# A two-block transformer on one core: how the end of each expert layer adds up its rows

## The chip, the cores and the metric

The kernel runs on one core of one Trainium2 chip. The metric is the device time of one execution in microseconds (us). The profiler's trace covers one execution; its engines are TensorE (PE, with its weight loads as PEld), VectorE (DVE), ScalarE (ACT), GpSimd (POOL) and SyncE (SP), which issues most DMAs.

## The reference, cut to what matters

512 tokens of width 1024 pass a first block (a state space mixer beside attention, then a convolutional feed-forward layer) and a second block of two layers. Layer 0 has gated linear attention, layer 1 sparse attention ("NSA"); each is followed by a mixture of 16 experts, of which a token uses two, and by layer norms:

```
for i in range(DEPTH_2):                       # 2 layers
    h = gla_mixer(x, ...) if i % 2 == 0 else nsa_mixer(x, ...)
    x = layer_norm(DN_ALPHA * x + h, ln_g[i, 0], ln_b[i, 0])
    f = moe_ffn(x, moe_w_router, moe_b_router, moe_w_gate[i], moe_w_up[i], moe_w_down[i])
    x = layer_norm(DN_ALPHA * x + f, ln_g[i, 1], ln_b[i, 1])

def layer_norm(x, g, b):
    mu = mean(x); var = mean(square(x - mu))
    return (x - mu) * rsqrt(var + LN_EPS) * g + b
```

In `moe_ffn` a token's two expert outputs are weighted and added. The change touches that sum and the layer norm behind it, the last line of the loop, in both layers.

## The kernel before, in words

The residual stream lies in SBUF as four row tiles `xt[0..3]` of 128 tokens x 1024 floats. The kernel is recorded through a framework with a scheduler that puts each engine's instructions in an order and adds the semaphores; buffers are pages of one arena (`pg`), the raw 1 MB weight pages being a ring of ten ("wr"). PSUM pool `p2` has three tiles of two banks (128x1024 floats), `p1` two of one bank.

The expert stage runs expert by expert. `up` makes the hidden rows, `turn` transposes them (`ht`), and `down` multiplies by the down weights into PSUM (`psy`, three matmuls for each product since numbers are split in a high and a low part; lines 394 to 396, operands split by an ACT cast and a DVE subtraction, line 369). Outputs of experts 0 to 13 are copied from PSUM (L1508) and scattered by GpSimd to DRAM, into `yd`, two rows of 1024 for each token. Experts 14 and 15 come too late for that way: their output is weighted on ACT (L1515) and stays in SBUF, with a 0/1 matrix `m` that says which token each row belongs to (`self.late`).

`combine` then makes z = residual + weighted rows + the two late experts. SP loads the rows `y` of each row tile from `yd` (L1459, four loads of 1 MB), behind the layer norm's gain and bias (L1165). On TensorE (L1574, L1581), in plain float32, a row tile gets identity x `xt`, `m14` x `yo14`, and where the tile is in `by_pe`, diag(weight) x `y` for both rows of a token (`dw`, made by DVE in L1540 to 1544); expert 15 comes last (L1581). `by_pe` is (0, 1) in layer 0 and (0, 1, 2, 3) in layer 1; the other tiles' rows are added on DVE beforehand by `mac`, two 128x1024 instructions (L1463). Then for each tile: `bn_stats` x2 and `bn_aggr` on DVE (L1591, L1592), a square root on ACT (L1593), a Newton step on DVE (L1600 to L430), and the scaling: in layer 0 on ACT (L1178), in layer 1 two DVE instructions with gain and bias (L1595, L1608) and the store of the output.

In layer 0 the next stage starts inside: `x4_tile` transposes a normalised tile (L1748), applies gain and bias while copying out of PSUM (L1756 on ACT, L1758 on DVE), splits it, and multiplies it by `w_n1` (tile name `n`); behind the four tiles the same input goes through `w_n2` and `w_n4` (tile name `tm`). `w1_split` splits the three pages of `w_n1` between the steps. DVE's order in `combine` is that of the code; the other engines' order is the scheduler's.

Of the kernel before, what the change touches and what calls it, by code (L numbers as in the profile page):

```python
# [268 lines left out]
def build(ctx, tc, I, out, dbg=None):  # L269
# [890 lines left out]

    def load_gb(gi):
        g_ = sb(2048, "lngb")
        gb = [g_[:, :1024], g_[:, 1024:]]
        for j in range(2):
            nc.sync.dma_start(out=gb[j], in_=I['lngb'][gi:gi + 1, j * 1024:(j + 1) * 1024].to_broadcast([P, 1024]))  # L1165
        return gb
# [24 lines left out]
    class Layer:  # L1191
        def __init__(self, l, by_pe):
            self.l, self.by_pe = l, by_pe
            self.xd = dr.tile([S, 1024], F32, tag=f"xd{l}", name=f"xd{l}")
            self.yd = dr.tile([2 * S, 1024], F32, tag=f"yd{l}", name=f"yd{l}")
# [300 lines left out]
        def down(self, e, hs):  # L1496
# [6 lines left out]
            for k in range(2):  # L1503
                for nh in range(2):
                    mm3(psy[:, nh], (hh[:, k * P:(k + 1) * P], hl[:, k * P:(k + 1) * P]), wt.next(512), k == 0, k == 1)
            yo = sb(1024, "ysb", bufs=3)
# [14 lines left out]
        def experts(self):  # L1521
# [31 lines left out]
            for t in reversed(range(4)):  # L1553
                ar.rings[f"y{t}"] = (4, [ar.rings["wr"][1].pop()])
            drop("gh", "gl", "hs", "hhl", "wr", "wh", "wl")
            wt.bufs = 2

        def combine(self, done=None, between=None):


            self.gb = load_gb(2 * self.l + 1)
            eps = small("epsl", (1,))
            V.memset(eps, LN_EPS / ALPHA ** 2)

            def early(t):

                ps = p2("late")
                for nh in range(2):
                    c = slice(nh * 512, (nh + 1) * 512)
                    a = [(ident, xt[t][:, c]), (self.late[0][0][:, t * P:(t + 1) * P], self.late[0][1][:, c])]  # L1570
                    if t in self.by_pe:
                        a += [(self.dw[:, t, k], self.y[t][:, k * 1024 + nh * 512:k * 1024 + (nh + 1) * 512]) for k in range(2)]
                    for i, (l_, r_) in enumerate(a):
                        TE.matmul(ps[:, nh], l_, r_, start=i == 0, stop=False)  # L1574
                if t in self.by_pe:
                    drop(f"y{t}")
                return ps

            def last(t):
                for nh in range(2):  # L1580
                    TE.matmul(z[t][:, nh], self.late[1][0][:, t * P:(t + 1) * P], self.late[1][1][:, nh * 512:(nh + 1) * 512], start=False, stop=True)  # L1581

            z = [early(0), early(1)]
            last(0)
            last(1)
            with tc.manual_schedule(engines={mybir.EngineType.DVE}):
                for t in range(5):
                    if t < 4:
                        bs, mv, rs = (small(n, (w,), bufs=2) for n, w in (("bs", 12), ("mv", 2), ("lrs", 2)))
                        for j in range(2):  # L1590
                            V.bn_stats(bs[:, 6 * j:6 * j + 6], z[t][:, j])  # L1591
                        V.bn_aggr(mv, bs)  # L1592
                        A.activation(rs[:, 0:1], mv[:, 1:2], AF.Sqrt, bias=eps)  # L1593
                        if not done:
                            V.scalar_tensor_tensor(v2(xt[t]), z[t], mv[:, 0:1], v2(self.gb[0]), op0=ALU.subtract, op1=ALU.mult)  # L1595
                        if between:
                            between(t)
                        if t < 2 and t + 2 not in self.by_pe:
                            self.mac(t + 2)
                        V.reciprocal(rs[:, 0:1], rs[:, 0:1])  # L1600
                        V.tensor_scalar(bs[:, 0:1], mv[:, 1:2], LN_EPS / ALPHA ** 2, -0.5, op0=ALU.add, op1=ALU.mult)
                        run(newton(rs[:, 0:1], bs[:, 0:1], bs[:, 1:2]))
                        if done:
                            V.scalar_tensor_tensor(rs[:, 1:2], mv[:, 0:1], -1.0, rs[:, 0:1], op0=ALU.mult, op1=ALU.mult)
                            normalize(v2(xt[t]), z[t], rs)
                        else:
                            for c in (slice(0, 1024),) if t < 3 else (slice(0, 512), slice(512, 1024)):
                                V.scalar_tensor_tensor(xt[t][:, c], xt[t][:, c], rs[:, 0:1], self.gb[1][:, c], op0=ALU.mult, op1=ALU.add)  # L1608
                                nc.sync.dma_start(out=out[t * P:(t + 1) * P, c], in_=xt[t][:, c])
                    if t > 0 and done:  # L1610
                        done(t - 1)
                    if t in (1, 2):
                        z.append(early(t + 1))
                        last(t + 1)
            drop("ysb", "xg")


# [79 lines left out]

    L0 = Layer(0, (0, 1))
    L0.start()
# [28 lines left out]
    def w1_split():  # L1728
        n = 1680 if len(w1) < 2 else 1120
        w1.append((sb(1680, "w1h", FR, 3)[:, :n], sb(1680, "w1l", FR, 3)[:, :n]))  # L1730
        for j in split(st.get()[:, :n], *w1[-1]):
            if len(w1) > 1:
                after(j, L0.last)

    w1_split()
    x4h, x4l = [], []
    kcd = dr.tile([S, 512], F32, tag="kcd", name="kcd")
# [355 lines left out]
```

## Time and profile before

| | |
|---|---|
| median of three runs | 1930.62 us (1928.56 to 1931.67) |
| the profiled execution | 1927.89 us, of which the span is 1925.8 us |
| busy: PE, PEld, DVE, ACT | 94%, 78%, 63%, 45% of the span |
| mean granted TensorE clock | 0.965 |
| layer 0's combine in the trace | about 1249 to 1328 us |
| layer 1's combine | about 1876 to 1922 us |

Times in the trace are microseconds from the start of the span; a row of the timeline has the start, the length, and in brackets how long the engine was idle before it and which instruction's end released it.

### The profile page before, as it was taken

What the parts mean: (1) busy time and instruction counts of PE and PEld (TensorE: products, weight loads), DVE (VectorE), ACT (ScalarE), POOL (GpSimd) and SP (SyncE); (2) the same over time, 40 slices, a digit from 0 to 9 for tenths busy, and PEclk for the clock granted to TensorE, in tenths of its full rate; (3) what the DMA queues carried; (4) which work ended last, traced back from release to release, by engine and by line L of the source; (5) the groups of instructions that cost most, each with busy time, mean ns of one, the idle gap of its engine ahead of it and who ended that gap; (6) DMA issues with size and microseconds to landing.
All of it is one profiled execution on the core that took longest, in us unless ns stands there. A gap on an engine that the chain in (4) does not pass through costs nothing. (4 is left out here: it accounts for less than half of the span.)

```text
span 1925.8 us, 27564 instructions
## 1 busy us (share of the span) xinstructions
PE 1806.3 (94%) x10879; PEld 1506.3 (78%) x10879; DVE 1211.6 (63%) x2304; ACT 874.9 (45%) x1394; POOL 148.6 (8%) x128
## 2 busy tenths in 40 slices
PE   8899999899999999999999699979998999869997
PEld 7899877798899888877888588748886777748873
DVE  7755358776555543235348789954437777678994
ACT  4233346433333322243214388834225665638880
POOL 2310000021000000000000122200000000012220
PEclk9999999899999999999989799989998999879999
DMA  5434222242222232372226599552241002639953
GB/s 193 113 115 136 83 88 66 67 159 105 88 88 102 96 123 104 111 254 89 88 66 241 193 328 380 214 220 82 78 136 40 2 1 88 237 144 330 381 212 130
DMA packets 68279, 277.87 MB, mean 144 GB/s; under 512 B 21923, under 2 KB 24499, under 8 KB 42032
## 3 DMA queue, kind: packets, MB, share of 16 engines
q1 hardware_dynamic: 52032, 255.30, 37.1%
q0 software_dynamic: 8640, 16.00, 2.2%
q10 hardware_dynamic: 7472, 4.76, 1.1%
q8 instruction: 87, 1.43, 0.3%
q14 instruction: 48, 0.39, 0.1%
HBM read 258.01 MB, written 37.24 MB: 153 GB/s over the span
## 5 line engine op out<-in xcount | busy, mean ns | idle before, releaser
L369 ACT CAST pg<-pg 128x1024 fp32r<-128x1024 f32 (+2 forms) x437 | 428.2, 1004 | 556.8 <-PE mm L395 224.4
L369 DVE TENSOR_TENSOR pg<-pg,pg 128x1024 fp32r<-128x1024 f32 (+2 forms) x437 | 504.2, 1176 | 278.3 <-ACT pg L369 264.7
L394 PE MATMUL mm<-pg,pg 128*128 128x258 f32 (+2 forms) x1504 | 483.8, 322 | 1.3 <-ACT pg L888 0.7
L396 PE MATMUL mm<-pg,pg 128*128 128x258 f32 (+2 forms) x1504 | 481.7, 321 | 3.3 <-DVE pg L369 3.3
L395 PE MATMUL mm<-pg,pg 128*128 128x258 f32 (+2 forms) x1504 | 481.6, 320 | 0.0
L394 PEld LDWEIGHTS mm<-pg,pg 128*128 128x128 f32 x1504 | 286.4, 191 | 27.7 <-ACT pg L886 2.7
L396 PEld LDWEIGHTS mm<-pg,pg 128*128 128x128 f32 x1504 | 285.7, 190 | 24.1 <-DVE pg L369 3.9
L395 PEld LDWEIGHTS mm<-pg,pg 128*128 128x128 f32 x1504 | 286.3, 190 | 21.2 <-issue 0.4
L360 DVE TENSOR_TENSOR pg<-mm,pg 128x256 f32<-128x256 f32 (+3 forms) x138 | 66.3, 510 | 137.9 <-PE mm L396 137.8
L394 PE MATMUL psh<-pg,pg 128*128 128x512 f32 x256 | 105.8, 413 | 7.1 <-ACT pg L369 7.1
L395 PE MATMUL psh<-pg,pg 128*128 128x512 f32 x256 | 105.8, 413 | 3.3 <-DVE pg L369 3.3
L396 PE MATMUL psh<-pg,pg 128*128 128x512 f32 x256 | 103.8, 406 | 0.2 <-DVE pg L369 0.2
L395 PE MATMUL tm<-pg,pg 128*128 128x512 f32 x192 | 76.7, 400 | 3.0 <-DVE pg L369 3.0
L396 PE MATMUL tm<-pg,pg 128*128 128x512 f32 x192 | 75.2, 392 | 0.0
L394 PE MATMUL tm<-pg,pg 128*128 128x512 f32 x192 | 74.6, 399 | 0.3 <-ACT pg L369 0.3
L1990 ACT ACTIVATE pg<-ns,nmx 128x512 f32<-128x512 f32 (+3 forms) x128 | 66.3, 531 | 10.1 <-DVE nmx L1986 5.6
L360 DVE TENSOR_TENSOR pg<-pg,pg 128x512 f32<-128x512 f32 (+11 forms) x99 | 52.3, 549 | 23.7 <-ACT pg L675 9.4
L394 PEld LDWEIGHTS psh<-pg,pg 128*128 128x128 f32 x256 | 49.9, 195 | 18.5 <-ACT pg L369 8.3
L1986 DVE TENSOR_REDUCE nmx<-ns 128x2 f32<-128x1024 f32 (+3 forms) x48 | 50.0, 1042 | 19.2 <-PE ns L1983 19.0
L395 PEld LDWEIGHTS psh<-pg,pg 128*128 128x128 f32 x256 | 49.9, 195 | 15.1 <-DVE pg L369 4.8
L360 DVE TENSOR_TENSOR pg<-pg 128x64 f32<-128x64 f32 (+8 forms) x127 | 48.5, 403 | 17.4 <-ACT pg L1033 15.4
L396 PEld LDWEIGHTS psh<-pg,pg 128*128 128x128 f32 x256 | 49.6, 194 | 11.1 <-DVE pg L369 0.8
(460 smaller groups left out, 3018.0 us busy)
## 6 DMA issues: line engine op xcount, KB each, us to landing
pg<-in_w_moe_dram SPq DMA_DIRECT2D x96, 1024.0 KB
pg<-in_w_up_dram SPq DMA_DIRECT2D x22, 1024.0 KB
pg<-in_w_dn_dram SPq DMA_DIRECT2D x11, 1024.0 KB
pg<-in_w_g_dram SPq DMA_DIRECT2D x8, 1024.0 KB
yd<-zd SPq DMA_DIRECT2D x16, 512.0 KB
pg<-in_w_go_dram SPq DMA_DIRECT2D x8, 1024.0 KB
pg<-yd SPq DMA_DIRECT2D x8, 1024.0 KB
pg<-in_w_n_dram SPq DMA_DIRECT2D x8, 1024.0 KB
```

The lines of the kernel that those rows point to most:

```text
L360: return (eng or V).tensor_tensor(o, a, b, op=op)
L369: return A.copy(h, src), V.tensor_tensor(l, src, h.bitcast(F32), op=ALU.subtract)
L394: TE.matmul(o, a[0], b[0], start=start, stop=False)
L395: TE.matmul(o, a[0], b[1], start=False, stop=False)
L396: return TE.matmul(o, a[1], b[0], start=False, stop=stop)
L1986: V.tensor_reduce(mx, sc, axis=AX.X, op=ALU.max, negate=True)
L1990: A.activation(pp[:, r, br], sc[:, r, br], AF.Exp, bias=mx[:, r, br:br + 1], accum_out=se[:, r, br:br + 1])
```

## The change

All four row tiles of both layers now get their rows by `mac` on DVE; `by_pe` and `dw` are gone. TensorE multiplies only the two late experts (`late_rows`), ordered behind the last `psy` matmul. In layer 0 the residual stays on DVE, which adds the PSUM tile into `xt` (`add`), takes its statistics from SBUF and normalises from SBUF. The last layer has a function of its own, `combine_last`: TensorE adds the residual by the identity, ACT makes the sum of z, the sum of (z - mean)^2 and its root, DVE the scalings. In layer 0 the three loads of `w_n1` are issued ahead of the row loads and gain and bias behind them. The gain and bias of `xt` itself (`affine`) is ordered behind the last split of `x4_tile`.

```diff
@@ class Layer, experts
-                if e == 14:
-                    self.dw = self.xg[2].rearrange("p (t k n) -> p t k n", t=4, k=2)
-                    for t in self.by_pe:
-                        tt(self.dw[:, t], ident.unsqueeze(1).to_broadcast([P, 2, P]), bc(self.wts[:, :, t], P), ALU.mult)
+            early = 0
+            if self.l == 0:
+                st.ahead(3)
+                early = 3
+            else:
+                self.load_gb2()
+                early = 1
             for t in range(4):
                 self.y.append(sb(2048, "wr", F32, WM))
                 ld = self.load(t, self.y[t])
...
+        def late_rows(self, t, ps, own=False):
+            for i, (m, yo) in enumerate(self.late):
+                for nh in range(2):
+                    c = slice(nh * 512, (nh + 1) * 512)
+                    last = TE.matmul(ps[nh], m[:, t * P:(t + 1) * P], yo[:, c], start=i == 0, stop=i == 1 and not own)
+                    after(last, self.done_by)
+                    if own and i == 1:
+                        TE.matmul(ps[nh], ident, xt[t][:, c], start=False, stop=True)
...
+            def add(t):
                 for nh in range(2):
+                    z = xt[t][:, nh * 512:(nh + 1) * 512]
+                    tt(z, z, ps[t][nh], ALU.add)
+            ps = [late(t) for t in range(3)]
             with tc.manual_schedule(engines={mybir.EngineType.DVE}):
+                self.mac(0)
                 for t in range(5):
                     if t < 4:
+                        add(t)
...
-                            V.bn_stats(bs[:, 6 * j:6 * j + 6], z[t][:, j])
+                            V.bn_stats(bs[:, 6 * j:6 * j + 6], xt[t][:, 512 * j:512 * (j + 1)])
...
+                        if t < 3:
+                            self.mac(t + 1)
+                        self.root(rs[:, 0:1], mv[:, 1:2], bs)
+                        V.scalar_tensor_tensor(rs[:, 1:2], mv[:, 0:1], -1.0, rs[:, 0:1], op0=ALU.mult, op1=ALU.mult)
+                        normalize(xt[t], xt[t], rs)
+                    between(t)
+                    if t > 0:
                         done(t - 1)
+                    if t == 1:
+                        ps.append(late(3))
...
+        def combine_last(self):
...
+            def total(t):
+                z[t] = p2("late")
+                self.late_rows(t, [z[t][:, 0], z[t][:, 1]], True)
+                A.activation(v2(waste), z[t], AF.Copy, accum_out=ss[:, t:t + 1])
+            def mean(t):
+                V.tensor_scalar(nm[:, t:t + 1], ss[:, t:t + 1], -1.0 / D, None, op0=ALU.mult)
+                A.activation(v2(waste), z[t], AF.Square, bias=nm[:, t:t + 1], accum_out=ss[:, 4 + t:5 + t])
+                A.activation(rs[:, t:t + 1], ss[:, 4 + t:5 + t], AF.Sqrt, scale=1.0 / D, bias=eps)
+            with tc.manual_schedule(engines={mybir.EngineType.DVE}):
+                self.mac(0)
+                self.mac(1)
+                total(0)
+                total(1)
+                mean(0)
+                for t in range(4):
+                    V.scalar_tensor_tensor(v2(xt[t]), z[t], nm[:, t:t + 1], v2(self.gb[0]), op0=ALU.add, op1=ALU.mult)
+                    if t < 2:
+                        self.mac(t + 2)
+                        total(t + 2)
+                    if t < 3:
+                        mean(t + 1)
+                    r, v = rs[:, t:t + 1], ss[:, 4 + t:5 + t]
+                    V.tensor_scalar(v, v, 1.0 / D, None, op0=ALU.mult)
+                    self.root(r, v, b[:, 2 * t:2 * t + 2])
+                    for c in (slice(0, 1024),) if t < 3 else (slice(0, 512), slice(512, 1024)):
+                        V.scalar_tensor_tensor(xt[t][:, c], xt[t][:, c], r, self.gb[1][:, c], op0=ALU.mult, op1=ALU.add)
+                        nc.sync.dma_start(out=out[t * P:(t + 1) * P, c], in_=xt[t][:, c])
...
@@ x4_tile and behind it
-            split(f[:, hf], x4h[t][:, hf], x4l[t][:, hf])
+            x4_last.append(split(f[:, hf], x4h[t][:, hf], x4l[t][:, hf])[1].ins.name)
...
-        affine(xt[t], L0.gb, V)
+        for i in affine(xt[t], L0.gb, V):
+            after(i, x4_last[-1])
```

First place: SP's loads at the start of layer 0's combine, before. `lngb` is gain and bias, `yd` the rows, 128x1680 the pages of `w_n1`, 128x2048 those of `w_n2` and `w_n4`.

```order
L334 DMA pg_92<-in_w_moe_dram 128x2048
L1165 DMA pg_8640<-in_lngb_dram 128x1024 x2
L1459 DMA pg_94<-yd_7634 128x2048
L1459 DMA pg_96<-yd_7634 128x2048
L1459 DMA pg_7171<-yd_7634 128x2048
L1459 DMA pg_7110<-yd_7634 128x2048
L334 DMA pg_8638<-in_w_n_dram 128x1680
L334 DMA pg_92<-in_w_n_dram 128x1680
L334 DMA pg_102<-in_w_n_dram 128x1680
L334 DMA pg_8638<-in_w_n_dram 128x2048
L334 DMA pg_92<-in_w_n_dram 128x2048
L334 DMA pg_102<-in_w_n_dram 128x2048
```

The same loads in the changed kernel:

```order
L334 DMA pg_96<-in_w_n_dram 128x1680
L334 DMA pg_7171<-in_w_n_dram 128x1680
L1460 DMA pg_7110<-yd_7634 128x2048
L1460 DMA pg_102<-yd_7634 128x2048
L1460 DMA pg_7119<-yd_7634 128x2048
L1460 DMA pg_7628<-yd_7634 128x2048
L1165 DMA pg_8638<-in_lngb_dram 128x1024 x2
L1836 DMA pg_132<-in_w_c_dram 128x384
L1836 DMA pg_132<-in_c_ropec_dram 128x64
L1836 DMA pg_132<-in_c_pe_dram 128x16
L334 DMA pg_7628<-in_w_n_dram 128x2048
L1822 DMA kcd<-pg_6402 128x512
```

The three `w_n1` loads moved from behind the rows to ahead of them, gain and bias from ahead to behind, and two small loads stand ahead of the next weights.

Second place: TensorE around the last expert's `psy` in layer 0, before (a row with x2 is two instructions).

```order
L1499 MATMUL ht<-c_ident,pg_7017 128x128 x2
L394 MATMUL psy<-pg_430,pg_8987 128x512
L395 MATMUL psy<-pg_430,pg_8987 128x512
L1574 MATMUL late<-pg_7017,c_ident 128x512
L1574 MATMUL late<-pg_132,pg_7064 128x512
L1574 MATMUL late<-pg_132,c_ident 128x512
L1574 MATMUL late<-pg_132,pg_7064 128x512
L396 MATMUL psy<-pg_430,pg_8987 128x512
L394 MATMUL psy<-pg_430,pg_8987 128x512
L395 MATMUL psy<-pg_430,pg_8987 128x512
L396 MATMUL psy<-pg_430,pg_8987 128x512
L394 MATMUL psy<-pg_483,pg_8987 128x512
```

And in the changed kernel, from the last `psy` on, with `x4T` the transposes and `late_10259`, `late_10260` two one-bank tiles:

```order
L394 MATMUL psy<-pg_483,pg_8987 128x512
L395 MATMUL psy<-pg_483,pg_8987 128x512
L396 MATMUL psy<-pg_483,pg_8987 128x512
L1576 MATMUL late<-pg_132,pg_7064 128x512 x2
L1576 MATMUL late<-pg_7094,pg_7064 128x512 x2
L1576 MATMUL late<-pg_132,pg_7064 128x512 x2
L1576 MATMUL late<-pg_7094,pg_7064 128x512 x2
L1576 MATMUL late<-pg_132,pg_7064 128x512 x2
L1576 MATMUL late<-pg_7094,pg_7064 128x512 x2
L1799 MATMUL x4T<-c_ident,pg_7017 128x128 x8
L1576 MATMUL late_10259<-pg_132,pg_7064 128x512
L1576 MATMUL late_10260<-pg_132,pg_7064 128x512
```

The four float32 matmuls inside `psy` are gone; three row tiles of four matmuls each follow it, then the first transposes.

Third place: DVE at the end of the kernel with the semaphores that an instruction waits for, in the changed kernel from the first `mac` on. L1464 is `mac`, L1643 the mean's sign, L1654 the scaling by the gain that reads PSUM (`late`), L1664 the last one.

```order
L1464 SCALAR_TENSOR_TENSOR pg_7017<-pg_10699,wts,pg_7017 128x1024 [waits DMAHW0_49]
L1464 SCALAR_TENSOR_TENSOR pg_7017<-pg_10699,wts,pg_7017 128x1024 [waits DVE_49]
L1464 SCALAR_TENSOR_TENSOR pg_132<-pg_11453,wts,pg_132 128x1024 [waits DMAHW1_49]
L1464 SCALAR_TENSOR_TENSOR pg_132<-pg_11453,wts,pg_132 128x1024 [waits DVE_49]
L1643 TENSOR_SCALAR lnm<-lss 128x1 [waits Activation_49]
L1654 SCALAR_TENSOR_TENSOR pg_7017<-late,lnm,pg_7628 128x1024 [waits DMAHW6_49,PE_49,Activation_49]
L1464 SCALAR_TENSOR_TENSOR pg_7060<-pg_11524,wts,pg_7060 128x1024 [waits DMAHW2_49]
L1464 SCALAR_TENSOR_TENSOR pg_7060<-pg_11524,wts,pg_7060 128x1024 [waits DVE_49]
L1643 TENSOR_SCALAR lnm<-lss 128x1
L1661 TENSOR_SCALAR lss<-lss 128x1 [waits Activation_49]
L1585 RECIPROCAL lrt<-lrt 128x1
L1586 TENSOR_SCALAR lbs<-lss 128x1 [waits DVE_49]
```

And ACT there, from the weighting of expert 15 on: L1640 is the sum, L1644 the squares, L1645 the root.

```order
L1517 ACTIVATE pg_6402<-psy,sw 128x1024 [waits DMASW6_49,PE_49]
L1640 ACTIVATE pg_7017,lss<-late 128x1024 [waits DMASW1_49,PE_49]
L1640 ACTIVATE pg_7017,lss<-late 128x1024 [waits PE_49,Activation_49]
L1644 ACTIVATE pg_7017,lss<-late,lnm 128x1024 [waits DVE_49,Activation_49]
L1645 ACT_TABLE_LOAD
L1645 ACTIVATE lrt<-lss,epsl 128x1 [waits Activation_49]
L1640 ACTIVATE pg_7017,lss<-late 128x1024 [waits PE_49]
L1644 ACTIVATE pg_7017,lss<-late,lnm 128x1024 [waits DVE_49,Activation_49]
L1645 ACTIVATE lrt<-lss,epsl 128x1 [waits Activation_49]
L1640 ACTIVATE pg_7017,lss<-late 128x1024 [waits PE_49]
L1644 ACTIVATE pg_7017,lss<-late,lnm 128x1024 [waits DVE_49,Activation_49]
L1645 ACTIVATE lrt<-lss,epsl 128x1 [waits Activation_49]
```

The `mac` of tiles 2 and 3 stands behind the first and second L1654, each of which waits for PE and for ACT; the second L1643 reads ACT's sum of tile 1 without a wait of its own.

## Rows read from the trace of the kernel before

**Rows 1.** The page, engines: busy us (share of the span) and instructions.

```profile
PE 1806.3 (94%) x10879; PEld 1506.3 (78%) x10879; DVE 1211.6 (63%) x2304; ACT 874.9 (45%) x1394; POOL 148.6 (8%) x128
```

**Rows 2.** Timeline of PE, layer 0: start, length, instruction, [idle before <-releaser].

```profile
1254.20 1.02 PE L1574 MATMUL late<-pg,c_ident 128*128 128x512 f32 x2
...
1259.94 1.88 PE L1574 MATMUL late<-pg,pg 128*128 128x512 f32 x4
...
1271.95 1.88 PE L1581 MATMUL late<-pg,pg 128*128 128x512 f32 x4
1278.75 1.97 PE L1748 MATMUL x4T<-c_ident,pg 128*128 128x128 f32 x8 [4.92 <-ACT pg L1178]
1287.84 0.60 PE L394 MATMUL n<-pg,pg 128*128 128x280 f32 x1 [7.12 <-ACT pg L369]
...
1296.10 0.38 PE L396 MATMUL n<-pg,pg 128*128 128x280 f32 x1
...
1302.46 0.40 PE L394 MATMUL n<-pg,pg 128*128 128x280 f32 x1
...
1328.54 0.39 PE L394 MATMUL tm<-pg,pg 128*128 128x512 f32 x1
```

**Rows 3.** Timeline of DVE, layer 0.

```profile
1270.38 3.73 DVE L369 TENSOR_TENSOR pg<-pg,pg 128x1680 fp32r<-128x1680 f32 x2 [1.84 <-ACT pg L369]
1274.03 2.60 DVE L1463 SCALAR_TENSOR_TENSOR pg<-pg,wts,pg 128x1024 f32<-128x1024 f32 x2
1276.54 0.16 DVE L1600 RECIPROCAL lrs<-lrs 128x1 f32<-128x1 f32 x1
...
1285.26 0.72 DVE L1758 TENSOR_SCALAR pg<-x4T,lnfm 128x128 f32<-128x128 f32 x2
1287.31 0.73 DVE L1758 TENSOR_SCALAR pg<-x4T,lnfm 128x128 f32<-128x128 f32 x2 [1.33 <-ACT pg L1756]
```

**Rows 4.** Timeline of ACT, layer 0.

```profile
1272.58 1.12 ACT L369 CAST pg<-pg 128x1120 fp32r<-128x1120 f32 x1 [0.49 <-DMA pg<-in_w_n_dram]
1277.49 1.21 ACT L1178 ACTIVATE pg<-late,lrs 128x1024 f32<-128x1024 f32 x1 [3.79 <-DVE lrs L1604]
```

**Rows 5.** Timeline of SP: issues of the row loads in both layers.

```profile
1250.90 2.30 SPq L1459 DMA_DIRECT2D pg<-yd  x4
...
1876.65 2.00 SPq L1459 DMA_DIRECT2D pg<-yd  x4
```

**Rows 6.** Windows: PE, PEld, DVE, ACT, POOL busy (instructions), clock, DMA share, GB/s.

```profile
1278.00:1280.00 2.00, 1.25 (x6) 1.25 (x7) 1.97 (x5) 0.99 (x2) 0.00 (x0) 0.55 0.74 311
...
1290.00:1292.00 2.00, 2.00 (x4) 0.80 (x3) 0.00 (x0) 0.00 (x0) 0.00 (x0) 0.54 0.00 0
...
1878.00:1880.00 2.00, 1.39 (x4) 0.86 (x5) 0.54 (x2) 0.56 (x2) 0.00 (x0) 1.00 0.86 332
1880.00:1882.00 2.00, 2.00 (x6) 0.95 (x5) 0.00 (x0) 0.00 (x0) 0.00 (x0) 1.00 1.01 422
...
1920.00:1922.00 2.00, 0.00 (x0) 0.00 (x0) 1.89 (x7) 0.00 (x0) 0.00 (x0) 0.50 0.00 0
```

**Rows 7.** Timeline of PE, end of the kernel.

```profile
1886.29 1.13 PE L1574 MATMUL late<-pg,c_ident 128*128 128x512 f32 x2 [1.20 <-ACT pg L1515]
...
1915.58 1.88 PE L1581 MATMUL late<-pg,pg 128*128 128x512 f32 x4
```

**Rows 8.** Timeline of DVE, end of the kernel.

```profile
1895.17 1.30 DVE L1591 BATCH_NORM_STATS2 bs<-late 128x6 f32<-128x512 f32 x2 [16.16 <-PE late L1581]
...
1920.96 1.42 DVE L1608 SCALAR_TENSOR_TENSOR pg<-pg,lrs,pg 128x512 f32<-128x512 f32 x2
```

**Rows 9.** Groups of like operations: duration ns min/median/max; and busy us, mean ns.

```profile
L1667 ACT ACTIVATE pg<-go x4: 1024/1024/1027, 988.2 to 1019.4; 128x1024 f32<-128x1024 f32 x4
...
L1990 ACT ACTIVATION_READ_ACCUMULATOR pg<-ns,nmx 128x1 f32 x128 | 26.5, 207 | 0.0
...
L360 DVE TENSOR_TENSOR pg<-mm,pg 128x512 f32<-128x512 f32 x38 | 25.9, 690 | 39.1 <-PE mm L396 39.1
```

More of the change, by code (lines that the diff above doesn't have):

```diff
@@ L1158, in build, with load_gb @@
     sr = [sb(2048, "sr", bufs=2) for _ in range(2)]
-    def load_gb(gi):
+    def load_gb(gi, behind=None):
         g_ = sb(2048, "lngb")
@@ L1164, in load_gb @@
         for j in range(2):
-            nc.sync.dma_start(out=gb[j], in_=I['lngb'][gi:gi + 1, j * 1024:(j + 1) * 1024].to_broadcast([P, 1024]))
+            ld = nc.sync.dma_start(out=gb[j], in_=I['lngb'][gi:gi + 1, j * 1024:(j + 1) * 1024].to_broadcast([P, 1024]))
+            if behind:
+                after(ld, behind)
         return gb
@@ L1180, in affine @@
     def affine(z, gb, eng):
-        tt(z, z, gb[0], ALU.mult, eng)
-        tt(z, z, gb[1], ALU.add, eng)
+        return tt(z, z, gb[0], ALU.mult, eng), tt(z, z, gb[1], ALU.add, eng)
     def run(steps, n=None):
@@ L1191, in build, with __init__ @@
     class Layer:
-        def __init__(self, l, by_pe):
-            self.l, self.by_pe = l, by_pe
+        def __init__(self, l):
+            self.l = l
             self.xd = dr.tile([S, 1024], F32, tag=f"xd{l}", name=f"xd{l}")
@@ L1504, in down @@
                 for nh in range(2):
-                    mm3(psy[:, nh], (hh[:, k * P:(k + 1) * P], hl[:, k * P:(k + 1) * P]), wt.next(512), k == 0, k == 1)
+                    i = mm3(psy[:, nh], (hh[:, k * P:(k + 1) * P], hl[:, k * P:(k + 1) * P]), wt.next(512), k == 0, k == 1)
+            self.done_by = i.ins.name
             yo = sb(1024, "ysb", bufs=3)
@@ L1554, in experts, with load_gb2 @@
                 ar.rings[f"y{t}"] = (4, [ar.rings["wr"][1].pop()])
+            for i in reversed(range(early)):
+                ar.rings[f"ahead{i}"] = (4, [ar.rings["wr"][1].pop()])
             drop("gh", "gl", "hs", "hhl", "wr", "wh", "wl")
             wt.bufs = 2
-        def combine(self, done=None, between=None):
-            self.gb = load_gb(2 * self.l + 1)
+        def load_gb2(self):
+            g_ = sb(2048, "wr", F32, WM)
+            self.gb = [g_[:, :1024], g_[:, 1024:]]
+            for j in range(2):
+                nc.sync.dma_start(out=self.gb[j], in_=I['lngb'][3:4, j * 1024:(j + 1) * 1024].to_broadcast([P, 1024]))
@@ new lines, in late_rows @@
+        def late_rows(self, t, ps, own=False):
[6 more added lines that the diff above has]
+                        TE.matmul(ps[nh], ident, xt[t][:, c], start=False, stop=True)
+            self.done_by = last.ins.name
+            return ps
@@ L1562, in combine, with root, late @@
+        def root(self, rs, var, b):
+            V.reciprocal(rs, rs)
+            V.tensor_scalar(b[:, 0:1], var, LN_EPS / ALPHA ** 2, -0.5, op0=ALU.add, op1=ALU.mult)
+            run(newton(rs, b[:, 0:1], b[:, 1:2]))
+        def combine(self, done, between):
+            self.gb = load_gb(2 * self.l + 1, st.behind)
             eps = small("epsl", (1,))
             V.memset(eps, LN_EPS / ALPHA ** 2)
-            def early(t):
+            def late(t):
+                if t == 3:
+                    return self.late_rows(t, [p1("late1"), p1("late1")])
@@ L1567, in early @@
                 ps = p2("late")
+                return self.late_rows(t, [ps[:, 0], ps[:, 1]])
+            def add(t):
                 for nh in range(2):
[L1569 to L1585, printed above, removed]
+                    z = xt[t][:, nh * 512:(nh + 1) * 512]
+                    tt(z, z, ps[t][nh], ALU.add)
@@ L1592, in combine @@
                         V.bn_aggr(mv, bs)
                         A.activation(rs[:, 0:1], mv[:, 1:2], AF.Sqrt, bias=eps)
[L1594 to L1609, printed above, removed]
@@ L1610, in combine @@
-                    if t > 0 and done:
+                        if t < 3:
[5 more added lines that the diff above has]
+                    if t > 0:
                         done(t - 1)
-                    if t in (1, 2):
-                        z.append(early(t + 1))
-                        last(t + 1)
+                    if t == 1:
+                        ps.append(late(3))
@@ L1615, in combine @@
             drop("ysb", "xg")
+        def combine_last(self):
+            eps = small("epsl", (1,))
+            V.memset(eps, LN_EPS / ALPHA ** 2)
+            nm, ss, rs, b = (small(n, (w,)) for n, w in (("lnm", 4), ("lss", 8), ("lrt", 4), ("lbs", 8)))
+            waste, z = self.xg[2], {}
+            def total(t):
[25 more added lines that the diff above has]
+                        nc.sync.dma_start(out=out[t * P:(t + 1) * P, c], in_=xt[t][:, c])
@@ L1696, in gla_norm @@
         return x
-    L0 = Layer(0, (0, 1))
+    L0 = Layer(0)
     L0.start()
@@ L1733, in w1_split @@
                 after(j, L0.last)
+        drop(f"ahead{len(w1) - 1}")
     w1_split()
-    x4h, x4l = [], []
+    x4h, x4l, x4_last = [], [], []
     kcd = dr.tile([S, 512], F32, tag="kcd", name="kcd")
@@ L2019, in values @@
                               pts[r][:, br, c * P:(c + 1) * P], start=False, stop=br == 1 and c == i)
-    L1 = Layer(1, (0, 1, 2, 3))
+    L1 = Layer(1)
     L1.start()
@@ L2074, in build @@
     L1.experts()
-    L1.combine()
+    L1.combine_last()
 def kernel(**inputs):
```

3 lines of the change are left out of this document (2 added, 1 removed).

## The prediction

> **What bounds the kernel now.** First the page's engine totals: TensorE is busy 94% of the span, DVE 63%, ACT 45% [rows 1]. So a change gains where TensorE stands idle or does work that another engine can do in its shadow, and DVE has room only on average. Then TensorE's timeline at the two places that the diff touches. In layer 0 the reader is to see two stops: 4.92 us ahead of the first transposes, released by ACT's normalising, and 7.12 us ahead of the first `n` matmul, released by an ACT cast [rows 2]; these 12 us are the largest stops there. Before them stands a float32 block from 1259.94 to 1273.8 (the last row's 1271.95 + 1.88), and four more float32 matmuls sit at 1254.20 inside `psy`. At the end, TensorE does nothing but float32 products from 1886.29 to 1917.46 [rows 7], while DVE waits 16.16 us for the first tile and finishes 4.9 us after TensorE [rows 8]. There TensorE is the bound; in layer 0 it is a chain over PE, DVE and ACT.
>
> **Price of a float32 matmul.** Layer 1 has ten of 128x512 for each row tile, forty in all, four of them ahead of 1886.29. The other 36 fill 1886.29 to 1917.46 [rows 7], 0.86 us each.
>
> **Layer 0, step by step.** The rows are issued at 1250.90 [rows 5]. In layer 1 the same loads were issued at 1876.65, 0.66 MB had moved by 1880 (332 GB/s x 2 us) and the rest of the first MB needs 0.9 us at 422 GB/s [rows 6]: last byte 4.3 us after issue, and up to 1.7 us more until a waiting engine sees it. I take 5.8 us (bounds 4.3 and 6.0): first rows at 1256.7, each further MB 2.5 us. The `w_n1` loads, 13 us behind the rows' place in the queue today (the last cast still waits 0.49 us for them at 1272.58 [rows 4]), now go into pages that are free earlier, while the DMA queues idle; cost nothing, and the 3.73 us of splits come one by one between the steps.
>
> `psy` loses four matmuls (3.4 us) and ends about 1256.1. Late products of tiles 0 to 2 are 12 x 0.86 = 10.3 us, tile 0 ready at 1259.6. DVE: `mac` 2.6 [rows 3] to 1259.2; `add` 2 x 0.69 [rows 9] from 1259.7 to 1260.9; statistics 1.3 [rows 8] to 1262.4; the second `mac` 2.5, then the root chain 0.86 (1276.54 to 1277.4 [rows 3]) to 1265.7; ACT normalises in 1.2 [rows 4]. First transposes at 1267, against 1278.75: 11.7 us earlier. Then DVE has, ahead of the copies out of the transposes, split 1.9, add 1.3, statistics 1.4, `mac` 2.5, root 0.9, split 1.2 (1120 columns against 1680) = 9.2 us, to 1275; from DVE's first copy to the first `n` matmul it takes 2.6 us today (1285.26 to 1287.84 [rows 2, 3]). So `n` starts at 1277.7, 10.1 us earlier.
>
> TensorE will have been idle from 1271.4 to 1277.7. Today 4.92 us of idling were followed by the clock at its lower level (0.55 in 1278 to 1280), which lasted until about 4 us after steady work had begun at 1287.84 (0.54 in 1290 to 1292) [rows 2, 6]. I charge the same: 4 us at half, 2 us lost. The rest of the first `n` tile is 6.2 us (1296.10 to 1302.3 [rows 2]), so it ends at 1287.2, against 1302.3: 15 us earlier, since the float32 block of tile 2 no longer stands inside it. Now the new wait: for each later tile, ACT's copies of the last `n` tile (0.8) stand ahead of the normalising (1.2), the second copy pair, DVE's and a split pair (0.7 + 0.7 + 0.7): TensorE idles some 3.5 us between tiles. Tile 1: 1290.7 + 1.0 + 6.2 = 1297.9; tile 2: 1301.6 to 1309.1; tile 3: 1310.0 to 1317.3, with 1.2 us of `tm` inside. Today `tm` starts at 1328.54 [rows 2]; like for like that is 1328.5 - 1316.1 = 12.4 us. The same sum over today's order comes out 2 us later than the trace at this point, so I take **13 us** (10 to 15).
>
> Does it stay? The second page of `w_n2` now is loaded only when tile 3's first DVE copies free its page, about 1307; 5.8 us later it is there, its splits stand behind `affine` (8 x 1.2 us), done at 1323, and TensorE wants it at 1327. Slack 4 us: nothing is charged, the lower bound covers it. Behind that TensorE is bound again, and carries the gain to layer 1's end.
>
> **Layer 1.** TensorE's block of 40 becomes 24 (8 x `m14`, 8 x `m15`, 8 x identity): 13.7 us less. But the order on DVE decides. `psy` ends at 1881.1 (3.4 us less, as above). Rows at 1882.5; `mac` of tiles 0 and 1 to 1885.0 and 1887.5; tile 0's identity products follow `mac`(0): z0 ready 1887.9, tile 1 at 1893.2 (six matmuls, 5.2 us). ACT has sum 0, sum 1, squares 0 in this order. A pass over 128x1024 from PSUM took 1.02 us, reading the accumulator 0.21 [rows 9]: 1.2 us each, so squares 0 are done at 1895.7. DVE's scaling L1654 of tile 0 waits for that, not for the mean alone (the sequence shows it waiting for ACT once more, and the next mean waiting for nothing), and **behind it in DVE's queue stands `mac`(2)**. 1895.7 + 1.2 (scaling) + 2.5 (`mac`) = 1899.4; identity and second half of tile 2, 2.7 us, 1902.1; sum and squares 2.4, 1904.6; scaling, `mac`(3), 3.7: 1908.4; TensorE 2.7, ACT 2.4: 1913.6; scaling of tile 2, sign, root and last step 3.4 to 1917; scaling of tile 3, root, last step 1.2 + 0.9 + 1.4 [rows 8] = 1920.6. Today the last step ends at 1922.38. Gain **1.8 us**. Each row tile costs 8.9 us round the loop where today it costs 6.9 on TensorE; only the earlier start pays. Bounds: sums and squares at 1.0 and 1.5 us give +2.6 and -0.1; rows 1.5 us later take 1.5; rows 0.8 earlier give +0.8. So -2 to +3.5. The ACT table load (1.3 us) falls behind squares 0, while ACT waits for `mac`(2): nothing.
>
> That L1654 waits for the squares, which only read the same PSUM tile, agrees with DVE's copies today: L1758 waits 1.33 us for ACT's L1756, a read of the same `x4T` [rows 3]. The Trainium skill (page "PSUM — Partial Sum Buffer", section "PSUM bank collisions raise a hardware error") says that ScalarE and VectorE must not read one bank at the same time, and that a scheduler therefore puts a dependency between them. By that rule the gain at the end is the 1.8 above; without it `mac`(2) would start 6 us earlier and the gain be 8.7.
>
> **Sum.** 13 + 1.8 = 14.8 us. The profiled execution's 1927.89 (1925.8 of it the span) gives 1913.1; it lies 2.7 under the median of the runs, so on the median 1930.62 - 14.8 = **1915.8**.
>
> **Rivals.** (a) The scaling doesn't wait for the squares: layer 1 gains 8.7, in all 21.7, 1909. For it: nothing needs the order by data. Against it: the waits named above. 12%. (b) Layer 0's gain isn't kept: the splits of `w_n2` come late, or TensorE's clock falls again in each of the 3.5 us stops between tiles (at the end it read 0.50 from 1920, 2.5 us after the last product [rows 6, 7]). Two more spells cost 2 us each, and `w_n2` 6 us late costs 2 beyond the slack: layer 0 gains 7, the end -1, in all 6, 1924.5. For it the windows, against it that TensorE's stops of 7 and 5 us today led to one spell only. 20%. (c) Slower: the lower clock level holds through both combines, since TensorE now idles in every tile. Price: each `n` tile 6.2 us more (24.8 in all, 2 charged, some hidden under DVE), so layer 0 ends 11 us later than today's; at the end 24 matmuls at 1.72 instead of 0.86 lengthen every step that waits for them, and the end loses 12. In all up to 23 slower, 1953; it decides once some 15 us of TensorE's work more than charged runs at half. Against it: today's spell ended while TensorE worked. 5%. (d) The loads don't come earlier, being held by the ring's pages, and DVE waits for `w_n1` as today: `n`(0) starts at 1280 instead, 2 to 3 us lost: 1918; a variant of the forecast.
>
> **How the numbers follow.** Forecast with (d) 63%: 1916, own range 1911 to 1921. (a) 12%, about 1909. (b) 20%, 1921 to 1929. (c) 5%. Range 1908 to 1926 leaves out a few per cent below and the worse part of (b) and all of (c) above. 0.2% (3.9 us) is about what a measurement can tell from no change: faster means under 1926.8. Forecast, (a) and most of (b) are: 0.84; same 0.10; slower 0.06.
>
> **What would show it.** Layer 0: `x4T` at about 1267, `n` at 1278, three stops of 3 to 4 us between `n` tiles released by ACT or DVE, `tm` some 13 us earlier. Layer 1: L1654 waiting on ACT's L1644, TensorE waiting on L1464 for tiles 2 and 3, the last L1664 ending only 1 to 3 us earlier relative to the last `ht` transposes. Wrong would be L1654 starting right behind the first L1643, or `tm` less than 8 us earlier.

## The result and the profile after

The changed kernel takes 1908.12 us (median of 7 runs, 1901.79 to 1917.12) against 1930.62 (7 runs, 1927.68 to 1934.04): ratio 0.9889, 95% interval 0.9862 to 0.9916, so 16 to 27 us faster. The forecast was 1916, range 1908 to 1926: right in direction, and inside the range by 0.12 us, with three of the seven runs below it. The profiled execution of the changed kernel took 1908.12 us, 1906.2 of it the span.

The page's engine totals of the changed kernel, to set beside [rows 1]:

```profile
PE 1785.2 (94%) x10815; PEld 1498.3 (79%) x10815; DVE 1223.5 (64%) x2314; ACT 883.7 (46%) x1410; POOL 142.8 (7%) x128
```

TensorE has 64 records and 21.1 us of work less (the trace has two records for each float32 matmul of 128x512, so that a row with x2 is one product), DVE 11.9 us and ACT 8.8 us more. To see where the time went, both traces are cut at the same instructions: the last expert's last `ht` transpose in layer 0 (1252.1 before, 1253.1 after; the second of a row's two), the first matmul of the compress stage (`cim`), the last `ht` transpose of layer 1, and the end of DVE's last instruction. These markers, before and then after:

```profile
1252.00 0.38 PE L1499 MATMUL ht<-c_ident,pg 128*128 128x128 f32 x2
...
1356.36 0.49 PE L1851 MATMUL cim<-c_ident,pg 32*128 32x32 f32 x5
...
1876.99 0.38 PE L1499 MATMUL ht<-c_ident,pg 128*128 128x128 f32 x2
```

```profile
1252.98 0.38 PE L1500 MATMUL ht<-c_ident,pg 128*128 128x128 f32 x2
...
1342.14 0.49 PE L1904 MATMUL cim<-c_ident,pg 32*128 32x32 f32 x5
...
1856.85 0.38 PE L1500 MATMUL ht<-c_ident,pg 128*128 128x128 f32 x2
```

All in us; "first x4T" and "first n" are counted from the first marker.

| stretch | before | after | forecast of the gain | gain |
|---|---|---|---|---|
| up to layer 0's last ht | 1252.1 | 1253.1 | 0 | -1.0 |
| ... to the first x4T | 26.6 | 14.7 | 11.7 | 11.9 |
| ... to the first n matmul | 35.7 | 24.4 | 10.1 | 11.3 |
| layer 0: last ht to compress | 104.25 | 89.04 | 13 | 15.2 |
| compress to layer 1's last ht | 520.7 | 514.8 | 0 | 5.9 |
| end: layer 1's last ht to DVE's end | 45.28 | 45.77 | 1.8 | -0.5 |

Timeline of TensorE in layer 0 of the changed kernel (start, length, instruction, idle before and what ended it), against [rows 2]:

```profile
1256.91 10.46 PE L1576 MATMUL late<-pg,pg 128*128 128x512 f32 x24
1267.83 1.09 PE L1799 MATMUL x4T<-c_ident,pg 128*128 128x128 f32 x8 [0.46 <-ACT pg L1180]
1268.76 3.60 PE L1576 MATMUL late<-pg,pg 128*128 128x512 f32 x8
1277.47 0.60 PE L394 MATMUL n<-pg,pg 128*128 128x280 f32 x1 [5.11 <-ACT pg L369]
...
1278.10 1.91 PE L1799 MATMUL x4T<-c_ident,pg 128*128 128x128 f32 x8
...
1281.91 0.43 PE L396 MATMUL n<-pg,pg 128*128 128x280 f32 x1
...
1287.14 0.29 PE L396 MATMUL n<-pg,pg 128*128 128x280 f32 x1
1290.60 0.60 PE L394 MATMUL n<-pg,pg 128*128 128x280 f32 x1 [3.18 <-ACT pg L369]
...
1300.89 0.40 PE L394 MATMUL n<-pg,pg 128*128 128x280 f32 x1
```

The float32 products of three tiles stand in one block, the first transposes come 0.46 us behind it, and the stop ahead of the first `n` matmul is 5.11 us. Behind the first `n` tile there is a second stop of 3.18 us, ahead of the third tile almost none. The matmuls of 0.43 us beside those of 0.29 show the clock, which the windows of that stretch give (columns as in [rows 6]):

```profile
1278.00:1280.00 2.00, 2.00 (x11) 1.99 (x10) 1.86 (x4) 0.38 (x1) 0.00 (x0) 0.50 0.00 0
...
1284.00:1286.00 2.00, 2.00 (x18) 2.00 (x17) 1.52 (x8) 0.00 (x0) 0.00 (x0) 1.00 0.42 61
...
1292.00:1294.00 2.00, 2.00 (x11) 2.00 (x10) 2.00 (x4) 2.00 (x4) 0.00 (x0) 0.50 0.00 0
```

0.50 is the lower level, 1.2 GHz. It is granted once behind the stop of 5.11 us and again behind that of 3.18.

The end of the changed kernel, TensorE's timeline first, against [rows 7]:

```profile
1863.35 1.02 PE L1579 MATMUL late<-pg,c_ident 128*128 128x512 f32 x2
...
1871.08 2.74 PE L1576 MATMUL late<-pg,pg 128*128 128x512 f32 x6
1877.58 2.08 PE L1579 MATMUL late<-pg,c_ident 128*128 128x512 f32 x2 [3.76 <-DVE lnm L1643]
...
1888.12 2.08 PE L1579 MATMUL late<-pg,c_ident 128*128 128x512 f32 x2 [3.70 <-DVE lnm L1643]
1889.99 1.92 PE L1576 MATMUL late<-pg,pg 128*128 128x512 f32 x2
1891.70 1.91 PE L1579 MATMUL late<-pg,c_ident 128*128 128x512 f32 x2
```

Then DVE's, against [rows 8]:

```profile
1860.40 5.12 DVE L1464 SCALAR_TENSOR_TENSOR pg<-pg,wts,pg 128x1024 f32<-128x1024 f32 x4 [2.08 <-DMA pg<-yd]
1867.27 0.15 DVE L1643 TENSOR_SCALAR lnm<-lss 128x1 f32<-128x1 f32 x1 [1.75 <-ACT pg L1640]
1873.72 1.28 DVE L1654 SCALAR_TENSOR_TENSOR pg<-late,lnm,pg 128x1024 f32<-128x1024 f32 x1 [6.29 <-ACT pg L1644]
1874.92 2.60 DVE L1464 SCALAR_TENSOR_TENSOR pg<-pg,wts,pg 128x1024 f32<-128x1024 f32 x2
...
1884.27 1.28 DVE L1654 SCALAR_TENSOR_TENSOR pg<-late,lnm,pg 128x1024 f32<-128x1024 f32 x1 [4.67 <-ACT pg L1644]
...
1901.32 1.41 DVE L1664 SCALAR_TENSOR_TENSOR pg<-pg,lrt,pg 128x512 f32<-128x512 f32 x2
```

And ACT's, which released it:

```profile
1871.34 1.02 ACT L1640 ACTIVATE pg<-late 128x1024 f32<-128x1024 f32 x1 [4.10 <-PE late L1579]
...
1872.48 1.11 ACT L1644 ACTIVATE pg<-late,lnm 128x1024 f32<-128x1024 f32 x1
1873.50 0.19 ACT L1644 ACTIVATION_READ_ACCUMULATOR pg<-late,lnm 128x1 f32 x1
```

Read the three together. Squares of tile 0 end at 1873.69; the scaling L1654 starts at 1873.72; only then come the rows of tile 2 (L1464, done at 1877.52), and TensorE, idle since 1873.82, starts tile 2's identity products at 1877.58. The profile names L1643 as the releaser, the short instruction that DVE starts at 1877.44, but what the product reads is what L1464 wrote. The product that takes 1.02 us at 1863.35 takes 2.08 at 1877.58: the clock is at its lower level again, behind this stop and behind the next:

```profile
1878.00:1880.00 2.00, 2.00 (x3) 0.75 (x3) 1.53 (x3) 0.00 (x0) 0.00 (x0) 0.50 0.00 0
...
1888.00:1890.00 2.00, 1.88 (x3) 0.85 (x4) 1.89 (x8) 0.00 (x0) 0.00 (x0) 0.50 0.00 0
```

### The profile page after: what moved, and what is told of

It reads as the page before. It is cut to its first block, busy times and chain, and to the rows that moved or that the text cites. A ratio compares the mean times of both kernels' runs of the same rounds, so it can differ in the third digit from the quotient of the medians.

```text
span 1906.2 us, 27465 instructions
## 1 busy us (share of the span) xinstructions
PE 1785.2 (94%) x10815; PEld 1498.3 (79%) x10815; DVE 1223.5 (64%) x2314; ACT 883.7 (46%) x1410; POOL 142.8 (7%) x128
## 5 line engine op out<-in xcount | busy, mean ns | idle before, releaser
L394 PEld LDWEIGHTS psh<-pg,pg 128*128 128x128 f32 x256 | 49.9, 195 | 18.6 <-ACT pg L369 8.3
## 6 DMA issues: line engine op xcount, KB each, us to landing
pg<-in_w_moe_dram SPq DMA_DIRECT2D x96, 1024.0 KB, 10.2
```

The costliest lines, as they stand in the source:

```text
L394: TE.matmul(o, a[0], b[0], start=start, stop=False)
```

## The experiments

Stretches as in the table above, each from one profiled execution; ratios are against the kernel before on the same chip (one chip for the first four runs, another for the last four). The untouched code up to layer 0's last `ht` ended between 1251.3 and 1266.0 us in the ten traces, so a stretch inside a trace tells a small effect better than a median does.

**Which layer carries the gain.** First run: layer 0 new, layer 1's end as before.

```
-    L1.combine_last()
+    L1.combine_old()
+  layer 1: identity * weights made on DVE again (dw), no load_gb2()
```

> The changed kernel with layer 1's end as it was (rows on TensorE, statistics on DVE), so only layer 0's half of the change is left. Theory: all of the gain comes from layer 0, and layer 1's half, read from the two traces, cost 0.5 us (45.4 us before, 45.9 after, from the last expert's ht transposes to the end of the last DVE step). Then this kernel is as fast as the changed one, 1906 to 1910 us, and its last 45.4 us look like those of before. Rival: layer 1's half carries 5 us or more of the 22, and this one stays at 1913 or above.

1910.76 us, ratio 0.9924 (0.9894 to 0.9955), between the two expectations and nearer the first; layer 0 88.9, end 45.26. Second run: layer 0 as before, layer 1's end new.

```
-    L1.combine()
+    L1.combine_last()
+  layer 1: load_gb2() in place of dw
```

> The kernel before with layer 1's end as changed (all rows on DVE, statistics on ScalarE), layer 0 untouched. Theory: within 2 us of the kernel before (1929 to 1932 us), since the earlier start of the late products is given back in the waits of TensorE for the row weighing of tiles 2 and 3, and in TensorE's lower clock there. Rival: 5 us or more faster.

1929.48 us, ratio 1.0017 (0.9996 to 1.0038); layer 0 104.6, end 45.90. TensorE's rows at that end repeat those of the changed kernel, the first stop for one:

```profile
1897.67 2.08 PE L1579 MATMUL late<-pg,c_ident 128*128 128x512 f32 x2 [3.76 <-DVE lnm L1603]
```

So layer 0 carries the gain, as far as totals can tell, and layer 1's half, with 13.7 us less of TensorE's work, brings nothing that a total shows.

**Is it the rows' place in DVE's queue?** All four tiles' rows weighed ahead of the first scaling:

```
-                self.mac(0)
-                self.mac(1)
+                for t in range(4):
+                    self.mac(t)
...
                     if t < 2:
-                        self.mac(t + 2)
                         total(t + 2)
```

> The changed kernel with the row weighing of tiles 2 and 3 moved on DVE ahead of the first scaling that reads PSUM; nothing else in the code is moved. Theory (these two steps stand queued behind scalings that wait for ScalarE's squares, and TensorE waits for them 3.7 us each and then runs at its lower clock): TensorE's 24 products run without a stop, 20.6 us, and the end from the ht transposes shrinks from 45.9 to 33 us, the kernel to about 1895 us. Rival (ScalarE's sums and squares, 2.8 us a tile, or the arrival of the rows are the bound): less than 4 us.

The end falls from 45.77 to 33.70 us, as expected: the two stops, 3.76 and 3.70 us, and the 4.3 us that the lower clock cost behind them (worked out below) make 11.8 of these 12.1. The kernel takes 1905.4 (1895.72 to 1910.58), ratio 0.9877 (0.9827 to 0.9927). The whole kernel missed its expected number, because its code ahead of layer 0's last `ht` took 13 us longer than in the changed kernel, in that execution. Next, on top of it, each tile's squares are issued ahead of the next tile's sum on ACT:

```
                 total(0)
-                total(1)
                 mean(0)
                 for t in range(4):
+                    if t < 3:
+                        total(t + 1)
...
-                    if t < 2:
-                        total(t + 2)
```

> As the kernel with the rows first, and each tile's squares issued on ScalarE ahead of the next tile's sum. Theory: one pass of ScalarE (1.3 us) and one scaling on DVE (1.2 us) leave the path behind the last product, so the end takes 30.5 us from the ht transposes, 2.5 less than with the rows first alone; about 1893 us. Rival: the order on ScalarE doesn't matter, since the last tile's sum and squares come after the last product in any order: no difference over 1 us.

End 31.27 us, 2.4 less than with the rows first alone, as expected; 1896.36 us (1894.97 to 1898.52), ratio 0.9845 (0.9807 to 0.9882). TensorE's timeline of that end, from the first identity product:

```profile
1866.72 1.02 PE L1579 MATMUL late<-pg,c_ident 128*128 128x512 f32 x2
...
1882.17 1.02 PE L1579 MATMUL late<-pg,c_ident 128*128 128x512 f32 x2
...
1883.88 1.02 PE L1579 MATMUL late<-pg,c_ident 128*128 128x512 f32 x2
```

And DVE's:

```profile
1863.63 10.16 DVE L1464 SCALAR_TENSOR_TENSOR pg<-pg,wts,pg 128x1024 f32<-128x1024 f32 x8 [1.93 <-DMA pg<-yd]
...
1875.12 1.28 DVE L1655 SCALAR_TENSOR_TENSOR pg<-late,lnm,pg 128x1024 f32<-128x1024 f32 x1 [1.27 <-ACT pg L1644]
```

From there on no row of TensorE waits, every identity product takes 1.02 us, and the last starts at 1883.88, where the changed kernel's starts at 1891.70 although its last `ht` was 3.4 us earlier. The scaling still waits for ACT's squares, but nothing that TensorE needs stands behind it.

**Are statistics on ScalarE worth it?** Rows first, and the statistics on DVE as before (`bn_stats`, `bn_aggr`), one scaling pass reading the mean:

```
-                A.activation(v2(waste), z[t], AF.Copy, accum_out=ss[:, t:t + 1])
-                A.activation(v2(waste), z[t], AF.Square, ...)
+                    for j in range(2):
+                        V.bn_stats(bs[:, 6 * j:6 * j + 6], z[t][:, j])
+                    V.bn_aggr(mv, bs)
```

> As the kernel with the rows first, but the last layer's mean and variance are taken on DVE as before (two bn_stats and a bn_aggr for each tile, from PSUM), so ScalarE has only the square roots. Theory: DVE then is the bound: 10.2 us of row weighing and 4 x 4.9 us of statistics and scaling behind the first rows make 33 to 34 us from the ht transposes, 2 to 3 more than the 31.3 with squares early on ScalarE. Rival: statistics on ScalarE are worth nothing or cost time (two passes of 1.2 us against 1.5 on DVE behind the last product): 31 us or less.

End 32.27 us, between the 33 to 34 expected and the rival's 31 or less; 1895.17 us (1890.45 to 1896.94), ratio 0.9824 (0.9805 to 0.9844). Statistics on ScalarE, in their best order, save 1.0 us of the stretch over those on DVE; the totals can't tell the two apart. Both beat the changed kernel: no run of either reaches its fastest, 1901.79. What pays at the end is the rows on DVE, if they come first.

**What pays in layer 0.** The changed kernel with the `w_n1` loads back behind the rows (the scheduler puts gain and bias behind the first of them):

```
             if self.l == 0:
-                st.ahead(3)
-                early = 3
+                pass
```

> The changed kernel with the three w_n1 loads behind the row loads again; the scheduler then puts gain and bias between them. Theory: DVE waits for the splits of w_n1, and layer 0's stretch from the last expert's ht transposes to the last n matmul grows from 62.3 us to about 67, so that the order of the loads carries a third of layer 0's gain, and the kernel takes about 1913 us. Rival: the loads are hidden by the rest, less than 1.5 us.

A miss. TensorE's stops in it:

```profile
1292.50 0.60 PE L394 MATMUL n<-pg,pg 128*128 128x280 f32 x1 [11.57 <-ACT pg L369]
...
1302.54 0.40 PE L394 MATMUL n<-pg,pg 128*128 128x280 f32 x1 [0.68 <-ACT pg L369]
```

The first `n` matmul is 7 us later (31.4 against 24.4 us from the marker), but the stop behind it shrinks from 3.18 us to 0.68, and the clock falls once in place of twice, mostly under the long stop (the lower level holds from 22.1 to 35.7 us behind the marker, the stop lasts from 19.9 to 31.4); layer 0 ends only 1.9 us later (90.9). The kernel took 1919.18 us (1917.27 to 1921.79), ratio 0.9958 (0.9942 to 0.9975): of its 10 us over the changed kernel, in the profiled executions, 8 lie ahead of layer 0's last `ht`, in code that the edit doesn't touch. Why all four runs are that slow stays open. The converse, the kernel before with the loads ahead and nothing else:

```
+            early = 0
+            if self.l == 0:
+                st.ahead(3)
+                early = 3
```

> The kernel before with nothing but the w_n1 loads ahead of the row loads. Theory: in layer 0 DVE splits the first page in the shadow of the late products and no longer waits 1.84 us for the second, so the stretch from the ht transposes to the last n matmul shrinks from 76.3 to about 72 us; the kernel takes about 1925 us. Rival: the two parts don't add up, and the loads alone give all or nothing of the 14 us.

A miss as well: 1929.1 us, ratio 1.0014 (0.9993 to 1.0035).

```profile
1286.46 0.60 PE L394 MATMUL n<-pg,pg 128*128 128x280 f32 x1 [8.34 <-ACT pg L369]
...
1317.05 0.40 PE L394 MATMUL n<-pg,pg 128*128 128x280 f32 x1 [3.14 <-ACT pg L369]
```

The first transposes come 4.6 us earlier, the first `n` matmul 4.2, and the second `n` tile still 3.9. Then it is given back: a stop of 3.14 us stands ahead of the third tile, where the kernel before has 0.15, and behind it the lower clock is granted once more, for 3.4 us; the last `n` matmul is 0.6 us later than before. On DVE, two splits of the next weights now stand between the last tile's statistics and its root, which the kernel before doesn't have there; the first of them:

```profile
1309.44 1.22 DVE L369 TENSOR_TENSOR pg<-pg,pg 128x1024 fp32r<-128x1024 f32 x1
```

So the rest of layer 0's half brings 13.3 of its 15.2 us without the loads; the loads bring 1.9 on top and nothing alone. What in that rest does it (the rows on DVE, the residual on DVE, the late experts' products in one block, the later `affine`), no run separates.

**Can the stop ahead of the first n tile go?** On the best end (squares early), DVE's last `w_n1` split and the copies out of the transposes go ahead of the next tile's rows and root:

```
                         A.activation(rs[:, 0:1], mv[:, 1:2], AF.Sqrt, bias=eps)
+                        if t == 1:
+                            between(t)
+                        if t > 0:
+                            done(t - 1)
                         if t < 3:
                             self.mac(t + 1)
...
-                    between(t)
-                    if t > 0:
+                    if t != 1:
+                        between(t)
+                    if t == 4:
                         done(t - 1)
```

> The kernel with squares early, and in layer 0 DVE does the last split of w_n1 and the copies out of each tile's transposes ahead of the next tile's row weighing and root. Theory: the first n matmul waits for DVE's queue, so it starts 3.4 us earlier; TensorE's stop ahead of it shrinks from 5.1 to under 2 us and the clock stays at its higher level in the first n tile: the stretch from ht to the last n matmul shrinks from 62.3 to 56 to 58 us, the kernel to about 1891 us. Rival: what the first tile gains the second gives back, since its row weighing and normalising come later: 61 us or more.

The rival was right. The first stop falls to 1.83 us and `n` starts 3.3 us earlier, but the last `n` matmul is 8 us later (70.5 against 62.3 from the marker), part of it because `tm` matmuls fill the gap ahead of it; the stretch up to the compress stage is 4.5 us longer (93.6 against 89.1):

```profile
1279.58 0.40 PE L394 MATMUL n<-pg,pg 128*128 128x280 f32 x1 [1.83 <-ACT pg L369]
...
1288.03 1.03 PE L1802 MATMUL x4T<-c_ident,pg 128*128 128x128 f32 x8
1292.07 0.60 PE L394 MATMUL n<-pg,pg 128*128 128x280 f32 x1 [3.01 <-ACT pg L369]
...
1306.75 0.60 PE L394 MATMUL n<-pg,pg 128*128 128x280 f32 x1 [5.66 <-ACT pg L369]
```

The second tile's transposes, which with squares early alone stand inside the first `n` tile, 25.0 us behind the marker, now come at 1288.03, 29.6 us behind it and behind that whole tile, since the rows and root that they wait for were put behind the copies. The third tile's come 3.4 us later and the fourth's 7.2. The second `n` tile still starts 3.9 us earlier, but the third 0.5 and the fourth 4.4 later; into the third's stop falls also an ACT cast of the next weights that waited for its load (at 1301.27), and how much of the loss is its, is not shown. 1905.22 us, ratio 0.9876 (0.9856 to 0.9897): 9 us more than with squares early alone, of which, in the profiled executions, 4.5 lie in layer 0, 2.3 between the combines and 2.0 ahead of the marker. A short first stop is worth nothing if the next tiles' chains pay for it.

## Why the prediction was right, and where its terms were off

**Layer 0 up to the first `n` matmul: right.** Transposes 14.7 us behind the marker (forecast 1267 - 1252.1 = 14.9), first `n` 24.4 (25.6), stop 5.11 (6.3), one spell of the lower clock until 1283, which cost the first `n` tile 2.8 us (2 charged).

**The stops between the `n` tiles: mis-sized, the total 2.2 us too small.** The sum had stops of 3.5, 3.7 and 0.9 us (with `tm` in the third), because ACT copies the last `n` tile out before it normalises a further tile and makes the next one's second copy pair. That holds ahead of the second `n` tile alone:

```profile
1287.46 0.39 ACT L1819 COPY pg<-n 128x280 f32<-128x280 f32 x1 [5.39 <-PE n L396]
...
1288.09 1.26 ACT L1180 ACTIVATE pg<-pg,lrs 128x1024 f32<-128x1024 f32 x1
...
1298.40 1.24 ACT L1180 ACTIVATE pg<-pg,lrs 128x1024 f32<-128x1024 f32 x1 [0.92 <-DVE lrs L1620]
...
1300.82 0.39 ACT L1819 COPY pg<-n 128x280 f32<-128x280 f32 x1
```

Counted from 0, tile 2 is normalised at 1288.09 behind the copies out of `n`(0), and `n`(1) waits for that; tile 3 at 1298.40, while TensorE was still at `n`(1), whose copies come behind. At the start of the last tile, `tm` matmuls filled the gap (five from 1308.36, then `n` at 1309.52). So the stops were 3.2, 0.1 and none, 4.8 us less; of the three stops that the forecast named as a sign, one came. Against that the second spell of the lower clock, which rival (b) named and the forecast left out, took 3.0: tile 1 ran from 1290.60 to 1300.79, 10.2 us where 7.2 were reckoned. With tile 0 ending 0.8 us earlier that makes 2.6, and the 12.4 of the sum, taken as 13, became 15.2.

**The end: the mechanism right, one term too small.** L1654 waits for ACT's squares, `mac`(2) and `mac`(3) stand behind it, TensorE waits for them, as the forecast said: the scaling starts 0.03 us after the accumulator read that closes the squares, though z was complete in PSUM at 1866.09 and its mean there from 1867.42, and by data the scaling needs nothing else but the gain, whose load was issued ahead of the rows'. The Trainium skill (page "PSUM — Partial Sum Buffer", section "PSUM bank collisions raise a hardware error") has the two engines kept apart on one bank. This trace agrees with it. Up to the squares of tile 0 the end came 1.9 us earlier than reckoned (16.7 us from the last `ht`, forecast 1895.7 - 1877.1 = 18.6), as the rows were there sooner (the first `mac` starts 3.4 us behind the last `ht`, forecast 1882.5 - 1877.1 = 5.4). Then scaling and rows took 3.8 us (3.7 reckoned), sum and squares 2.35 (2.4), but TensorE's three products behind each stop took 4.26 and 5.49 us (1877.58 to 1881.84, 1888.12 to 1893.61), not 2.7, at the lower clock. These 4.3 us turn 1.8 + 1.9 into -0.6; measured -0.5. The forecast had that only in its rivals (b) and (c). That stops are the cause fits the squares-early run, where the same products behind no stop take 1.02 us each.

**Rival (a), the scaling doesn't wait:** wrong as a mechanism. Its size, 8.7 us at the end, was to be had by moving the rows instead: 12.1 and 14.5 us. Its time, 1909, is nearer to the measured 1908.12 than the forecast's 1916; only the waits tell that it is the wrong one.

**Between the combines, put at nothing: 5.9 us in this pair of traces, of which the change can claim some 2.** Against the changed kernel's 514.8 us this stretch takes 515.9 with layer 1's end as before, 516.25 with layer 0 as before, and 516.7 with both as before and the loads ahead. Two differences repeat over the traces. The first is a spell of the lower clock in the compress stage. Windows of ten us around it, of before and then of after:

```profile
1384.00:1394.00 10.00, 10.00 (x70) 9.94 (x69) 3.32 (x6) 1.87 (x2) 0.00 (x0) 0.66 0.10 20
```

```profile
1370.00:1380.00 10.00, 10.00 (x82) 9.96 (x81) 3.01 (x5) 1.97 (x3) 0.00 (x0) 0.83 0.27 89
```

At two levels of 1 and 0.5, 0.66 means 6.8 us at the lower one and 0.83 means 3.4, so 1.7 us of work time. It is 6.8 us in the three traces with the old layer 0 (that with the loads ahead among them) and 3.4 in the five with the new one; 6.8 with the loads behind and 10.2 with the copies early show that layer 0's timing decides, not only its old or new form. The second is the missing `dw`. In layer 1's experts DVE made it ahead of a split that TensorE waits for; the row of before, then of after:

```profile
1858.80 0.50 PE L395 MATMUL psh<-pg,pg 128*128 128x512 f32 x1 [1.35 <-DVE pg L369]
```

```profile
1838.71 0.50 PE L395 MATMUL psh<-pg,pg 128*128 128x512 f32 x1 [0.27 <-DVE pg L369]
```

The stop is 1.35 us in the three traces whose layer 1 makes `dw` and 0.25 to 0.27 in the seven others. This 1.1 us is all that layer 1's half is seen to bring, and the forecast left it out. The remaining 4 us is a difference between the trace of before and the other traces with the old layer 0; its cause isn't shown. It and the layer 0 term are why the time fell at the range's edge: 15.2 + 5.9 - 0.5 - 1.0 = 19.6 in the two profiled executions, 22.5 between the medians, while the run with layer 0 alone has a ratio of 0.9924 (0.9894 to 0.9955), 9 to 20 us, around the 15.2 of its stretch. That the time still lies inside the range is luck, then, as much as the forecast's merit.

**Two readings of the prediction don't come out; its sum doesn't rest on them.** The 6.9 us that a row tile is said to cost on TensorE in the kernel before is the distance of DVE's statistics between the first three tiles; the fourth comes 8.6 us behind the third, and ten products at 0.86 are 8.6. And the chance of 0.84 holds 0.09 of rival (b)'s 0.20, which is not most of it.

## What to carry to other kernels

When an engine is made to wait for another, look at what stands behind the waiting instruction: here independent row work behind one wait cost 12.1 us, most of what taking 13.7 us of work off TensorE could have brought. Price TensorE's work behind each new stop at the lower clock as well as the upper one. An earlier first tile is worth nothing until the last tile's chain is earlier too, so try an edit alone and in reverse before it is credited. Work that is taken out of one place can show far from it: compare stretches between fixed instructions over several traces.

## What was not expected of the hardware

Stops as short as 3.18, 3.70 and 3.76 us were followed by the lower clock, where in layer 0's combine before one spell covered stops of 4.92 and 7.12. The same untouched code, up to layer 0's last `ht`, took 1251.3 to 1266.0 us over the profiled executions, and one kernel's runs spread over 15 us, wider than the difference in median between any kernel of the experiments and the one that it was edited from.
